# Placing a modulation's steps, the order of block couples, and the order of loads in the two MLPs of a fused block kernel

## The chip, the cores and the metric

The kernel runs on one core of a Trainium2 chip. A core has five engines with a queue of instructions each: PE (TensorE, matrix products), DVE (VectorE), ACT (ScalarE), POOL (GpSimd) and SP (SyncE, which here only issues DMAs). The metric is the time of one execution on the device in microseconds; lower is better. Several executions are timed and the median is given. A trace was taken of one of them.

## The reference, cut to what matters

Two transformer blocks follow each other on x of shape (1, 1024, 1024), all in float32. What the change touches is the MLP of each block, and the modulation vector of the second block:

```
# end of the first block
h = rmsnorm(x, g_mlp)
x = x + square(relu(h @ w_mlp_in)) @ w_mlp_out      # (1024,1024)x(1024,4096), (1024,4096)x(4096,1024)
x = rmsnorm(x, g_final)

# second block
mod = silu(c_2) @ w_ada_2 + b_ada_2                 # one row of 6 * 1024, cut in six:
sh1, sc1, gt1, sh2, sc2, gt2 = split(mod, 6)
x = x + gt1 * mixer(rmsnorm(x, g_mix_2) * (1 + sc1) + sh1)
h = rmsnorm(x, g_ffn_2) * (1 + sc2) + sh2
x = x + gt2 * (square(relu(h @ w_ff1_2)) @ w_ff2_2)
out = rmsnorm(x, g_final_2)
```

`mod` depends on inputs alone. It is first needed where the second block's first norm is made, at the end of the first MLP.

## The kernel before, in words

**Products.** Each float32 operand is split into a rounded part `hi` and a rest `lo` (`parts_of` for weights: a cast on ACT to `wh`, then a subtract on DVE, or on POOL where `eng=G`, to `wl`). `product` (L1231) adds up hi·hi, hi·lo and lo·hi over four chunks of 128: 12 matmuls of 128x128 by 128x512 into one PSUM bank.

**First GEMM of an MLP** (`mlp`, L1211). The hidden width of 4096 is cut into 16 couples m of two blocks of 128, the tokens into two halves of 512. A couple by two halves is a 2x2 block product, made in Winograd's form with seven products instead of eight. P1 and P2 (`first_two`, L1264) need only the first token half: P1 lands in `s1` (ACT copies it out), P2 plus `s1` gives `q11`, which is squared after a relu. The other five need operands made of both halves: T1 (in the place of the second half's first chunks), B22, and `t2`, `t3`, `t4` (six tiles of tag `q`). `make_t` (L1104) makes them on DVE, ACT and POOL when the second half's norm is known; its last part, `rest`, is called between two couples and holds four of the six PSUM banks. The norm itself comes from `begin[0]` (sum of squares, then a power on POOL, L127) and `begin[1]` (`spread`, L1035: four small PE transposes that lay the factor over the partitions).

Order in the code: P1, P2 of couples 0, 1, 2, with `begin[0]` and `begin[1]` between them, then `rest`, then couple 3; couples 2 and 3 split their weights on POOL. Then a loop over m: P5, then P1 and P2 of couple m + 1 (from m = 3 on), t2, B22, t3 and t4's products. `s1s` and `q11s` hold four couples. `sums` (L1279) makes the weights' sums of the next couple on POOL. Seven results per couple go to DRAM from ACT's queue (`save`).

**Modulation.** `ada` (L1182) is a Python generator: each `next` traces one step. For each of 12 column groups, eight steps load 128x512 of `w_ada_2` on SP's queue (`adaw`, two buffers) and multiply and add it on DVE into `ada`; then one empty step; then four PE transposes, a reduce and an add. `tick` calls it, only in the first MLP: four times per couple in the loop (L1312, L1331), once after it, and three times between products of the second GEMM (`tick2`, L1382).

**Second GEMM** (L1425). The hidden width comes in four quarters, each a 2x2 block product of seven products by four 128-wide blocks. `quarter` loads 1 MB of weights into a `q` tile, `second` loads 1 MB of stored results and splits it in four chunks (cast on ACT, subtract on DVE and POOL in turn, L1371). `upd` (L1374) adds a product to x, whose value was stored to DRAM before the MLP and is loaded back at L1356 in sixteen pieces, traced before all else of this stage. `U` and `V7` gather sums that are used twice. The x tiles are the same memory as `s1s`, `q11s` and the first GEMM's other results.

**What sets the order.** A planner of the framework lays the traced instructions out into one queue per engine: at each point it takes, of the instructions that its own estimate of time holds to be ready, the one traced first. So an instruction may be queued ahead of others traced before it, if it is thought ready sooner. Each engine then runs its queue strictly in that order, waiting on semaphores. A tile of a pool with n buffers can be given out again when the last reader of the tile n before it is done. `tc.issue_after(ins)` adds to each instruction traced inside it, on `ins`'s engine, the rule that it stands behind `ins` in the queue; it doesn't wait for `ins` to end.

Of the kernel before, what the change touches and what calls it, by code (L numbers as in the profile page):

```python
# [14 lines left out]
AF = mybir.ActivationFunctionType  # L15
# [4 lines left out]
P = 128  # L20
# [40 lines left out]
def block_kernel(ctx, tc, x, mem, positions, g_mix, w_in, b_gate, sinks, g_mem, w_mem_kv, w_proj_swa, w_proj_dsa,  # L61
# [50 lines left out]
    def tp_bank():  # L112
        return bank("tp")
# [1032 lines left out]

    xT = [hB([P, DC, 512], tag=n) for n in ("h_hi", "h_lo")]
# [30 lines left out]

    mod = cst([P, 48], tag="mod")
    bada = cst([P, 48], tag="bada")  # L1180

    def ada(modp):  # L1182
        badr = modp([48, P], tag="badr")
        nc.scalar.dma_start(badr, b_ada_2[0].rearrange("(k p) -> k p", p=P))
        pt = tp_bank()
        T.transpose(pt[:, :48], badr, ident[:48, :48])
        V.tensor_copy(bada, pt[:, :48])
        r0, _ = ROWS["c_2"]
        s_ = modp([P, 64], tag="silu")[:, :DC]
        A.activation(s_, cols[:, r0:r0 + 8], AF.Tanh, scale=0.5)  # L1190
        V.scalar_tensor_tensor(s_, s_, 1.0, cols[:, r0:r0 + 8], op0=OP.add, op1=OP.mult)
        V.tensor_scalar(s_, s_, 0.5, None, op0=OP.mult)
        for g in range(12):
            acc = modp([P, 512], tag="ada", bufs=1)
            for k in range(DC):
                w = modp([P, 512], tag="adaw", bufs=2)
                nc.sync.dma_start(w, w_ada_2[0, k * P:(k + 1) * P, halves(g)])
                if k == 0:
                    V.tensor_scalar(acc, w, s_[:, 0:1], None, op0=OP.mult)
                else:  # L1200
                    V.scalar_tensor_tensor(acc, w, s_[:, k:k + 1], acc, op0=OP.mult, op1=OP.add)
                yield
            yield
            m4 = mod[:, g * 4:(g + 1) * 4]
            pt = tp_bank()
            for j in range(4):
                T.transpose(pt[:, j * P:(j + 1) * P], acc[:, j * P:(j + 1) * P], ident)
            V.tensor_reduce(m4, pt.rearrange("p (j q) -> p j q", j=4), axis=AX.X, op=OP.add)
            V.tensor_tensor(m4, m4, bada[:, g * 4:(g + 1) * 4], op=OP.add)

    def mlp(PB, xt, d, w1, w2, scale, post, begin, middle, tick=lambda: None, gains=None, each=lambda i, e: None,  # L1211
# [52 lines left out]
        def first_two(m, e1, mid=None, eng=None):  # L1264
# [5 lines left out]
            if mid:  # L1270
                mid()
# [17 lines left out]
        first_two(0, w_of(wp, 0, "wr", 2))  # L1289
        begin[0]()  # L1290
        first_two(1, w_of(wp, 2, "wr", 2), begin[1])
        first_two(2, w_of(wp, 4, "wr", 2), eng=G)
        rest_t.pop()()
        begin[2]()
        first_two(3, w_of(wp, 6, "wr", 2), eng=G)
        e1s[0] = w_of(wep, 0, "we", 2)
        sums(0)
        for m in range(NM):
# [18 lines left out]
            V.tensor_tensor(q12, a, q12, op=OP.add)  # L1317
# [13 lines left out]
            for _ in range(2):  # L1331
                tick()
            a = mm_bank()
            product(a, u4, TQ["t4"])
            V.tensor_tensor(u3, a, u3, op=OP.add)
# [15 lines left out]
        tick()  # L1351
# [22 lines left out]
        def upd(hf, e, a, sl=slice(0, 512)):  # L1374
            t_ = xt[hf][:, e, sl]
            if scale is None:
                V.tensor_tensor(t_, a, t_, op=OP.add)
            else:
                V.scalar_tensor_tensor(t_, a, scale[:, e:e + 1], t_, op0=OP.mult, op1=OP.add)  # L1379
            return t_  # L1380

        def tick2():  # L1382
            for _ in range(3):
                tick()

        def gather(to, a, ch):
            if ch:
                V.tensor_tensor(to, a, to, op=OP.add)
            else:
                A.copy(to, a)  # L1390
# [34 lines left out]
        for ch in range(4):  # L1425
# [29 lines left out]
            tick2()  # L1455
# [13 lines left out]
            tick2()  # L1469
# [7 lines left out]
            tick2()  # L1477
# [8 lines left out]
            tick2()  # L1486
            if not last:
                b = second("q22", ch)
                for e, wt in blocks(a12):
                    a = mm_bank()  # L1490
                    product(a, wt, b)
                    upd(1, e, a)
                tick2()
# [39 lines left out]
    def post_mlp1(hf, st):  # L1533
        if hf == 0:
            for _ in ada_["it"]:
                pass
# [26 lines left out]
    ada_ = {}  # L1563

    def begin1():
        stp.close()
        ada_["it"] = ada(pools["mod"])
# [4 lines left out]
    def tick1():  # L1572
        next(ada_["it"], None)

    pools["mod"] = Pool("modp")
    mlp(hBp, xT, mlp_d, w_mlp_in[0], w_mlp_out[0], None, post_mlp1,
        (lambda: next(pend), lambda: next(pend), begin1), middle1, tick1, gsq)
    pools["mod"].close()
# [112 lines left out]
    pools["stm"].close()  # L1691
    pt = tp_bank()
# [405 lines left out]
```

## Time and profile before

| what | value |
|---|---|
| time, median of 3 (range) | 2725.16 us (2717.71 to 2726.5) |
| the profiled execution's own time | 2721.95 us |
| its span in the trace | 2720.2 us, 34915 instructions |
| PE, DVE, ACT, POOL busy | 2528.9, 1882.7, 1197.9, 988.1 us |
| mean granted clock of TensorE | 0.972 |
| first MLP in the trace | about 880 to 1610 us |
| second MLP in the trace | about 2037 us to the end |

Busy times are sums over the span; they overlap. Where PE is busy without a gap nothing else can shorten the time; where it is not, the idle time's releaser says what it waited for. A matmul's shown duration overlaps the next one's; how many of them fit into a stretch is the better measure.

### The profile page before, as it was taken

The page shows a single profiled execution, that of the slowest core. Times are in us where ns is not written, and L with a number is a line of the kernel's source. Part 1 is how long each engine was busy: PE and PEld are TensorE (multiplying, and loading weights), DVE is VectorE, ACT ScalarE, POOL GpSimd, SP SyncE. Part 2 cuts the span into 40 slices and gives each one's busy share as a digit, 9 for nine tenths or more (in the row PEclk, how much of TensorE's full clock was granted, in tenths as well). Part 3 has the DMA queues.
Part 4 walks back from the last instruction along what each step waited for, and adds up shares of the span by engine and source line. Part 5 has one row for each costly group of instructions (what it writes and reads, how often), then busy time and mean ns, then how long its engine had stood idle before and what let it go on. Part 6 is the DMA issues. An engine that isn't in the chain of part 4 may idle for free. (4 is left out here: it accounts for less than half of the span.)

```text
span 2720.2 us, 34915 instructions
## 1 busy us (share of the span) xinstructions
PE 2528.9 (93%) x12560; PEld 2107.4 (77%) x12560; DVE 1882.7 (69%) x3206; ACT 1197.9 (44%) x2218; POOL 988.1 (36%) x717
## 2 busy tenths in 40 slices
PE   7999999899999678888899979999997999989997
PEld 6899987788878566667688856888786788768886
DVE  7685878834455866676778896755658565578898
ACT  6575765335334433334433333323335554543433
POOL 3011123421002533333755661211334443476554
PEclk9999999999999889999999989999998999999999
DMA  3121022321155266666644301422343444753431
GB/s 114 53 61 40 25 79 90 89 61 41 63 183 179 78 203 200 202 204 230 220 170 155 109 24 51 156 63 70 120 152 97 160 150 159 250 204 134 170 109 62
DMA packets 275712, 338.57 MB, mean 124 GB/s; under 512 B 14268, under 2 KB 185044, under 8 KB 268372
## 3 DMA queue, kind: packets, MB, share of 16 engines
q1 hardware_dynamic: 234820, 253.65, 29.2%
q10 hardware_dynamic: 40720, 82.70, 8.3%
q8 instruction: 99, 1.62, 0.2%
q14 instruction: 73, 0.60, 0.1%
HBM read 250.25 MB, written 86.05 MB: 124 GB/s over the span
## 5 line engine op out<-in xcount | busy, mean ns | idle before, releaser
L1233 PE MATMUL mm<-h_hi,wh 128*128 128x512 f32 (+1 forms) x1136 | 455.5, 401 | 33.3 <-ACT wh L1227 17.2
L1235 PE MATMUL mm<-h_hi,wl 128*128 128x512 f32 (+1 forms) x1136 | 452.1, 398 | 10.5 <-DVE wl L1228 10.5
L1234 PE MATMUL mm<-h_lo,wh 128*128 128x512 f32 (+1 forms) x816 | 322.2, 395 | 0.0
L1233 PEld LDWEIGHTS mm<-h_hi,wh 128*128 128x128 f32 x1136 | 221.4, 195 | 82.2 <-ACT wh L1227 20.6
L1235 PEld LDWEIGHTS mm<-h_hi,wl 128*128 128x128 f32 x1136 | 220.7, 194 | 63.4 <-DVE wl L1228 18.2
L1227 ACT CAST wh<-q 128x1024 fp32r<-128x1024 f32 x116 | 121.7, 1052 | 331.7 <-PE mm L1234 297.7
L1234 PE MATMUL mm<-h_hi,wh 128*128 128x512 f32 (+1 forms) x624 | 244.8, 392 | 13.2 <-POOL h_hi L1371 13.2
L1228 DVE TENSOR_TENSOR wl<-q,wh 128x1024 fp32r<-128x1024 f32 x116 | 162.9, 1405 | 32.9 <-ACT wh L1227 31.3
L1234 PEld LDWEIGHTS mm<-h_lo,wh 128*128 128x128 f32 x816 | 158.3, 194 | 31.6
L1371 POOL TENSOR_TENSOR h_hi<-h_lo,h_hi 128x512 fp32r<-128x512 f32 x76 | 128.6, 1712 | 113.1 <-ACT h_hi L1370 107.9
L133 ACT CAST wh<-wr 128x1024 fp32r<-128x1024 f32 (+5 forms) x107 | 97.2, 911 | 149.7 <-PE mm L418 43.5
L1233 PE MATMUL mm<-q,wh 128*128 128x512 f32 x384 | 151.3, 394 | 10.4 <-DVE q L1119 10.4
L1235 PE MATMUL mm<-q,wl 128*128 128x512 f32 x384 | 150.2, 392 | 8.0 <-DVE wl L1228 8.0
L1234 PE MATMUL mm<-q,wh 128*128 128x512 f32 x384 | 150.9, 393 | 0.0
L1234 PEld LDWEIGHTS mm<-h_hi,wh 128*128 128x128 f32 x624 | 120.5, 193 | 37.9 <-POOL h_hi L1371 14.4
L1284 POOL TENSOR_TENSOR sa<-wr 128x512 f32<-128x512 f32 x32 | 41.7, 1303 | 264.8 <-DMA wr<-in_w_ff_dram 60.5
L134 POOL TENSOR_TENSOR wl<-wr,wh 128x1024 fp32r<-128x1024 f32 (+5 forms) x40 | 78.1, 1958 | 160.7 <-ACT wh L133 159.2
L1615 PE MATMUL mm<-h_hi,wh 128*128 128x512 f32 x320 | 132.0, 412 | 0.8 <-DVE kn L1648 0.8
L1617 PE MATMUL mm<-h_hi,wl 128*128 128x512 f32 x320 | 126.7, 396 | 0.0
L1371 DVE TENSOR_TENSOR h_hi<-h_lo,h_hi 128x512 fp32r<-128x512 f32 x76 | 120.4, 1605 | 8.3 <-ACT h_hi L1370 8.3
L1616 PE MATMUL mm<-h_lo,wh 128*128 128x512 f32 x320 | 125.5, 392 | 0.0
L1233 PE MATMUL mm<-h_lo,wh 128*128 128x512 f32 (+1 forms) x304 | 115.4, 380 | 0.6 <-ACT wh L1227 0.6
(589 smaller groups left out, 7006.9 us busy)
## 6 DMA issues: line engine op xcount, KB each, us to landing
h_lo<-ml_t SPq DMA_DIRECT2D x32, 1024.0 KB
adaw<-in_w_ada_dram SPq DMA_DIRECT2D x96, 256.0 KB
h_lo<-ml_q SPq DMA_DIRECT2D x24, 1024.0 KB
wr<-in_w_in_dram SPq DMA_DIRECT2D x42, 512.0 KB
wr<-in_w_out_dram SPq DMA_DIRECT2D x32, 512.0 KB
ml_t<-h_lo ACTq DMA_DIRECT2D x64, 256.0 KB
q<-in_w_mlp_out_dram SPq DMA_DIRECT2D x16, 1024.0 KB
ml_t<-x ACTq DMA_DIRECT2D x64, 256.0 KB
```

What stands on the lines that cost most here:

```text
L133: A.copy(hi, r)
L134: (eng or V).tensor_tensor(lo, r, raw(hi), op=OP.subtract)
L1227: A.copy(hi, r)
L1228: (eng or V).tensor_tensor(lo, r, raw(hi), op=OP.subtract)
L1233: mm(a, wt[0][:, k], b[0][:, k, sl], start=(k == 0), stop=False)
L1234: mm(a, wt[0][:, k], b[1][:, k, sl], start=False, stop=False)
L1235: mm(a, wt[1][:, k], b[0][:, k, sl], start=False, stop=(k == 3))
L1284: G.tensor_tensor(sa[:, 0:4], e2[:, 0:4], e2[:, 4:8], op=OP.add)
L1371: (G if c % 2 else V).tensor_tensor(lo[:, c], r[:, c], raw(hi[:, c]), op=OP.subtract)
L1615: mm(a, hi[:, k, :], r_hi, start=(k == 0), stop=False)
L1616: mm(a, hi[:, k, :], r_lo, start=False, stop=False)
L1617: mm(a, lo[:, k, :], r_hi, start=False, stop=(k == DC - 1))
```

## The change

It has four parts. (1) `ada` is moved up in the code and its pool opened earlier; its first two `next`s come in the projection before the first MLP, its loads are traced two steps ahead of their use, and each later `tick` gets an eviction on DVE and stands behind it. In the loop there are again four per couple, one behind each of four evictions; the other ticks follow evictions of the second GEMM's first three quarters. (2) P1 and P2 of couples 4, 5 and 6 come first, ahead of 0; their `s1` and `q11` go to DRAM (`away`) and are loaded back one iteration before their use; couples 0, then 1, 2, 3 follow, these three behind `rest`. Only couple 6 splits its weights on POOL. (3) In the second GEMM's first quarter the weights and the first two stored operands are traced ahead of the loads of x, which are four of 1 MB now. (4) In that quarter x is updated from the copied `U`, not from PSUM.

```diff
+        d["away"] = pool([P, 3, 2, 512], tag="ml_a")
...
     def ada(modp):
         badr = modp([48, P], tag="badr")
         nc.scalar.dma_start(badr, b_ada_2[0].rearrange("(k p) -> k p", p=P))
+        yield
...
+        yield
+        ld = []
+
+        def load(i):
+            if i < 12 * DC:
+                w = modp([P, 512], tag="adaw", bufs=2)
+                nc.sync.dma_start(w, w_ada_2[0, (i % DC) * P:(i % DC + 1) * P, halves(i // DC)])
+                ld.append(w)
+
+        load(0)
+        load(1)
         for g in range(12):
             acc = modp([P, 512], tag="ada", bufs=1)
             for k in range(DC):
-                w = modp([P, 512], tag="adaw", bufs=2)
-                nc.sync.dma_start(w, w_ada_2[0, k * P:(k + 1) * P, halves(g)])
+                w = ld.pop(0)
                 if k == 0:
                     V.tensor_scalar(acc, w, s_[:, 0:1], None, op0=OP.mult)
                 else:
                     V.scalar_tensor_tensor(acc, w, s_[:, k:k + 1], acc, op0=OP.mult, op1=OP.add)
+                load(g * DC + k + 2)
                 yield
...
+    def tick1(after):
+        with tc.issue_after(after.ins):
+            next(ada_, None)
...
         A.copy(xT[hf][:, e, :], pt)                      # x_cols, called for hf in 0, 1
+        if e == 2:
+            next(ada_)
...
             V.tensor_tensor(q11, a, s1, op=OP.add)       # first_two
             relu2(q11)
+            if away:
+                nc.scalar.dma_start(d["away"][:, m - 4, 0, :], s1)
+                nc.scalar.dma_start(d["away"][:, m - 4, 1, :], q11)
...
-        first_two(0, w_of(wp, 0, "wr", 2))
+        first_of(4, away=True)
         begin[0]()
-        first_two(1, w_of(wp, 2, "wr", 2), begin[1])
-        first_two(2, w_of(wp, 4, "wr", 2), eng=G)
+        first_of(5, away=True)
+        begin[1]()
+        first_of(6, eng=G, away=True)
+        first_of(0)
         rest_t.pop()()
         begin[2]()
-        first_two(3, w_of(wp, 6, "wr", 2), eng=G)
+        first_of(1)
+        first_of(2)
+        first_of(3)
...
-                if m >= 3:
+                if m >= 6:
                     first_two(m + 1, e1s[m + 1])
+                elif m >= 3:
+                    for i, t_ in enumerate((s1s, q11s)):
+                        nc.sync.dma_start(t_[(m + 1) % 4], d["away"][:, m - 3, i, :])
...
-            V.tensor_tensor(q12, p5, u2, op=OP.add)
-            for _ in range(2):
-                tick()
+            tick(V.tensor_tensor(q12, p5, u2, op=OP.add))
...
-            V.tensor_tensor(q12, a, q12, op=OP.add)
+            tick(V.tensor_tensor(q12, a, q12, op=OP.add))
...
-            V.tensor_tensor(q22, p5, u3, op=OP.add)
+            tick(V.tensor_tensor(q22, p5, u3, op=OP.add))
...
-            V.tensor_tensor(u3, a, u3, op=OP.add)
+            tick(V.tensor_tensor(u3, a, u3, op=OP.add))
...
-        for hf, es in ((1, range(4)), (0, range(8)), (1, range(4, 8))):
-            for e in es:
-                nc.sync.dma_start(xt[hf][:, e, :], d["x"][:, e, halves(hf)])
+        def x_back():
+            for hf, e0 in ((0, 0), (0, 4), (1, 0), (1, 4)):
+                nc.sync.dma_start(xt[hf][:, e0:e0 + 4, :], d["x"][:, e0:e0 + 4, halves(hf)])
...
+            if not late_ and e % 4 != 1 and (hf or e < 4):   # upd
+                tick(r)
...
+                if to is V7[0] or to is V7[2]:               # gather, from the second quarter on
+                    tick(r)
...
             b = second("q12", ch)
+            if not ch:
+                bt = second("t1", ch)
+                x_back()
             for e, wt in blocks(a11):
                 a = mm_bank()
                 product(a, wt, b)
                 gather(U[e], a, ch)
-                upd(1, e, a)
+                upd(1, e, a if ch else U[e])
             a12 = quarter(ch, 1, 0)
-            tick2()
-            b = second("t1", ch)
+            b = second("t1", ch) if ch else bt
...
-                V.tensor_tensor(U[e], a, U[e], op=OP.add)    # after t2's product
+                r = V.tensor_tensor(U[e], a, U[e], op=OP.add)
+                if e != 1:
+                    tick(r)
```

## Rows read from the trace of the kernel before

**Rows 1.** The page, part 1: busy us (share of the span) xinstructions.

```profile
PE 2528.9 (93%) x12560; PEld 2107.4 (77%) x12560; DVE 1882.7 (69%) x3206; ACT 1197.9 (44%) x2218; POOL 988.1 (36%) x717
```

**Rows 2.** Windows: length, busy us (count) of PE, PEld, DVE, ACT, POOL; PEclk, DMA share, GB/s.

```profile
880.00:930.00 50.00, 28.00 (x112) 21.77 (x111) 41.15 (x57) 23.41 (x40) 23.07 (x15) 0.79 0.24 74
930.00:1003.00 73.00, 59.22 (x247) 47.74 (x247) 52.84 (x63) 23.69 (x35) 33.67 (x22) 0.89 0.56 185
1003.00:1287.00 284.00, 252.05 (x1046) 198.04 (x1044) 200.84 (x261) 116.44 (x175) 102.15 (x72) 0.96 0.62 205
1287.00:1330.00 43.00, 27.96 (x102) 21.40 (x102) 23.03 (x23) 16.61 (x25) 30.88 (x14) 0.84 0.76 268
1330.00:1406.00 76.00, 76.00 (x337) 62.94 (x336) 63.09 (x65) 31.30 (x47) 46.97 (x23) 1.00 0.45 161
1406.00:1482.00 76.00, 76.00 (x337) 62.90 (x337) 64.43 (x65) 29.18 (x43) 45.50 (x22) 1.00 0.42 151
...
2037.00:2080.00 43.00, 27.03 (x114) 20.96 (x113) 37.92 (x51) 27.86 (x47) 21.01 (x14) 0.84 0.21 62
2080.00:2136.00 56.00, 52.76 (x217) 42.11 (x217) 32.59 (x39) 22.80 (x33) 30.44 (x22) 0.94 0.48 153
2136.00:2369.00 233.00, 232.92 (x1028) 192.55 (x1026) 132.25 (x164) 121.27 (x177) 100.49 (x73) 1.00 0.52 174
2369.00:2400.00 31.00, 19.51 (x67) 14.41 (x68) 17.29 (x17) 12.58 (x19) 23.07 (x11) 0.85 0.73 263
```

**Rows 3.** Waits of PE, 1003 to 1287: who waited for whom, total us, times, longest.

```profile
PE mm L1235 <- DVE wl L1228: 14.2, 16, 1.9
```

**Rows 4.** Waits of DVE, 1003 to 1287.

```profile
DVE ada L1201 <- DMA adaw<-in_w_ada_dram: 52.0, 30, 4.1
```

**Rows 5.** Groups of DVE, 1055 to 1230: count, busy us, mean ns, idle before, releaser.

```profile
L1201 DVE SCALAR_TENSOR_TENSOR ada<-adaw,silu,ada 128x512 f32<-128x512 f32 x50 | 40.5, 810 | 40.2 <-DMA adaw<-in_w_ada_dram 39.8
...
L1209 DVE TENSOR_TENSOR mod<-mod,bada 128x4 f32<-128x4 f32 x7 | 8.7, 1249 | 0.0
...
L1310 DVE TENSOR_TENSOR h_hi<-mm,h_hi 128x512 f32<-128x512 f32 x8 | 5.5, 684 | 0.0
```

**Rows 6.** Timeline of SP's queue: start us, us, what, count (merged).

```profile
1092.93 10.26 SPq L1197 DMA_DIRECT2D adaw<-in_w_ada_dram  x5
```

**Rows 7.** Timelines of ACT and DVE at the second MLP's start.

```profile
2051.79 1.05 ACT L1227 CAST wh<-sa 128x1024 fp32r<-128x1024 f32 x1
...
2080.54 1.20 DVE L1228 TENSOR_TENSOR wl<-sa,wh 128x1024 fp32r<-128x1024 f32 x1
```

**Rows 8.** Timelines of DVE, POOL and PE at the first MLP's start.

```profile
891.48 1.23 DVE L126 TENSOR_SCALAR st_r<-st_b 128x4 f32<-128x4 f32 x1
...
889.11 1.71 POOL L1284 TENSOR_TENSOR sa<-wr 128x512 f32<-128x512 f32 x1
...
897.96 1.02 POOL L127 TENSOR_TENSOR st_r<-st_r,mhalf 128x4 f32<-128x4 f32 x1
...
899.03 1.12 PE L1035 MATMUL tp<-ident,st_r 128*128 128x128 f32 x4 [10.23 <-POOL st_r L127]
```

**Rows 9.** Waits of PE, 1287 to 1330, and timelines of SP and ACT ahead of it.

```profile
PE mm L1234 <- POOL h_hi L1371: 7.4, 1, 7.4
PE mm L1233 <- ACT wh L1227: 6.0, 1, 6.0
...
1284.91 0.47 SPq L1407 DMA_DIRECT2D q<-in_w_mlp_out_dram  x1
...
1291.90 1.04 ACT L1227 CAST wh<-q 128x1024 fp32r<-128x1024 f32 x1 [7.49 <-DMA q<-in_w_mlp_out_dram]
```

**Rows 10.** Tile `ada`, 880 to 1345: duration ns min/median/max, first and last start.

```profile
L1201 DVE SCALAR_TENSOR_TENSOR ada<-adaw,silu,ada x84: 732/752/1803, 888.0 to 1232.2; 128x512 f32<-128x512 f32 x84
```

**Rows 11.** Groups of DVE and of POOL, 1330 to 1482.

```profile
L1371 DVE TENSOR_TENSOR h_hi<-h_lo,h_hi 128x512 fp32r<-128x512 f32 x19 | 33.7, 1799 | 0.0
...
L1450 POOL TENSOR_TENSOR q<-q,q 128x1024 f32<-128x1024 f32 x4 | 12.4, 3120 | 0.0
```

More of the change, by code (lines that the diff above doesn't have):

```diff
@@ L1145, in make_t, with ada @@
         rest_t.append(rest)
+    mod = cst([P, 48], tag="mod")
+    bada = cst([P, 48], tag="bada")
+    def ada(modp):
+        badr = modp([48, P], tag="badr")
+        nc.scalar.dma_start(badr, b_ada_2[0].rearrange("(k p) -> k p", p=P))
+        yield
+        pt = tp_bank()
+        T.transpose(pt[:, :48], badr, ident[:48, :48])
+        V.tensor_copy(bada, pt[:, :48])
+        r0, _ = ROWS["c_2"]
+        s_ = modp([P, 64], tag="silu")[:, :DC]
+        A.activation(s_, cols[:, r0:r0 + 8], AF.Tanh, scale=0.5)
+        V.scalar_tensor_tensor(s_, s_, 1.0, cols[:, r0:r0 + 8], op0=OP.add, op1=OP.mult)
+        V.tensor_scalar(s_, s_, 0.5, None, op0=OP.mult)
+        yield
[7 more added lines that the diff above has]
+        load(1)
+        for g in range(12):
+            acc = modp([P, 512], tag="ada", bufs=1)
+            for k in range(DC):
+                w = ld.pop(0)
+                if k == 0:
+                    V.tensor_scalar(acc, w, s_[:, 0:1], None, op0=OP.mult)
+                else:
+                    V.scalar_tensor_tensor(acc, w, s_[:, k:k + 1], acc, op0=OP.mult, op1=OP.add)
+                load(g * DC + k + 2)
+                yield
+            yield
+            m4 = mod[:, g * 4:(g + 1) * 4]
+            pt = tp_bank()
+            for j in range(4):
+                T.transpose(pt[:, j * P:(j + 1) * P], acc[:, j * P:(j + 1) * P], ident)
+            V.tensor_reduce(m4, pt.rearrange("p (j q) -> p j q", j=4), axis=AX.X, op=OP.add)
+            V.tensor_tensor(m4, m4, bada[:, g * 4:(g + 1) * 4], op=OP.add)
+    modp = Pool("modp", side="right")
+    ada_ = ada(modp)
+    def tick1(after):
+        with tc.issue_after(after.ins):
+            next(ada_, None)
     xT = [hB([P, DC, 512], tag=n) for n in ("h_hi", "h_lo")]
@@ L1176, in block_kernel, with mlp @@
     HT[1] = h_tiles(hBp)
[L1179 to L1195, printed above, removed]
-                w = modp([P, 512], tag="adaw", bufs=2)
-                nc.sync.dma_start(w, w_ada_2[0, k * P:(k + 1) * P, halves(g)])
[L1198 to L1211, printed above, removed]
+    def mlp(PB, xt, d, w1, w2, scale, post, begin, middle, tick=lambda ins: None, gains=None, each=lambda i, e: None,
             parts=((0, 0, 512), (1, 0, 512))):
@@ L1262, in save_later, with first_two @@
                 save(*later.pop(0))
-        def first_two(m, e1, mid=None, eng=None):
+        def first_two(m, e1, eng=None, away=False):
             s1, q11 = s1s[m % 4], q11s[m % 4]
@@ L1287, in sums, with first_of @@
             G.tensor_tensor(e1[:, 4:8], e1[:, 4:8], sa[:, 4:8], op=OP.subtract)
-        first_two(0, w_of(wp, 0, "wr", 2))
+        def first_of(m, **kw):
+            first_two(m, w_of(wp, 2 * m, "wr", 2), **kw)
+        first_of(4, away=True)
         begin[0]()
-        first_two(1, w_of(wp, 2, "wr", 2), begin[1])
-        first_two(2, w_of(wp, 4, "wr", 2), eng=G)
+        first_of(5, away=True)
+        begin[1]()
+        first_of(6, eng=G, away=True)
+        first_of(0)
         rest_t.pop()()
         begin[2]()
-        first_two(3, w_of(wp, 6, "wr", 2), eng=G)
+        first_of(1)
+        first_of(2)
+        first_of(3)
         e1s[0] = w_of(wep, 0, "we", 2)
@@ L1327, in mlp @@
             V.tensor_tensor(u3, a, u2, op=OP.add)
-            V.tensor_tensor(q22, p5, u3, op=OP.add)
+            tick(V.tensor_tensor(q22, p5, u3, op=OP.add))
             relu2(q22)
             save("q22", m, q22)
-            for _ in range(2):
-                tick()
             a = mm_bank()
             product(a, u4, TQ["t4"])
-            V.tensor_tensor(u3, a, u3, op=OP.add)
+            tick(V.tensor_tensor(u3, a, u3, op=OP.add))
             A.activation(u3, u3, AF.Relu)
@@ L1376, in upd @@
             if scale is None:
-                V.tensor_tensor(t_, a, t_, op=OP.add)
+                r = V.tensor_tensor(t_, a, t_, op=OP.add)
             else:
-                V.scalar_tensor_tensor(t_, a, scale[:, e:e + 1], t_, op0=OP.mult, op1=OP.add)
-            return t_
-        def tick2():
-            for _ in range(3):
-                tick()
+                r = V.scalar_tensor_tensor(t_, a, scale[:, e:e + 1], t_, op0=OP.mult, op1=OP.add)
+            if not late_ and e % 4 != 1 and (hf or e < 4):
+                tick(r)
+            return t_
         def gather(to, a, ch):
             if ch:
-                V.tensor_tensor(to, a, to, op=OP.add)
+                r = V.tensor_tensor(to, a, to, op=OP.add)
+                if to is V7[0] or to is V7[2]:
+                    tick(r)
             else:
@@ L1534, in post_mlp1 @@
         if hf == 0:
-            for _ in ada_["it"]:
+            for _ in ada_:
                 pass
@@ L1561, in h2_half @@
         yield
-    ada_ = {}
     def begin1():
         stp.close()
-        ada_["it"] = ada(pools["mod"])
     def middle1():
         pools["stm"] = Pool("stm", side="right", n512=2)
-    def tick1():
-        next(ada_["it"], None)
-    pools["mod"] = Pool("modp")
     mlp(hBp, xT, mlp_d, w_mlp_in[0], w_mlp_out[0], None, post_mlp1,
         (lambda: next(pend), lambda: next(pend), begin1), middle1, tick1, gsq)
-    pools["mod"].close()
     drm.close()
@@ L1691, in block_kernel @@
     pools["stm"].close()
+    modp.close()
     pt = tp_bank()
```

8 lines of the change are left out of this document (removed).

## The prediction

> **What bounds the kernel now.** I read the page first, then windows cut at the stages of the two MLPs, then the waits of PE and DVE inside them, then timelines at the two starts and the two hand-overs. PE is busy 93% of the span [rows 1], so a change pays only where PE is not. The windows [rows 2] say where that is: in the second GEMM PE runs 337 matmuls in 76.00 us without a gap, 0.2255 us each. That is my unit: a stretch has lost its length less 0.2255 us per matmul.
>
> The first GEMM is one computation done twice. The first MLP, from 930 to 1287, has 247 + 1046 PE instructions in 357 us; 48 are the small transposes of the modulation, so 1245 matmuls or 280.7 us: 76 us lost. The second MLP, from 2080 to 2369, runs the same 217 + 1028 = 1245 in 289 us: 8 us lost. Only the first carries the modulation steps, so these and what follows from them cost 76 - 8 = 68 us. PE waits there for weight splits of DVE [rows 3], and DVE in turn has stood 52.0 us, 30 times, at the head of its queue for `adaw` from DRAM, 4.1 us at worst [rows 4]. In 175 us (seven couples) DVE made 50 accumulating steps, over seven a couple [rows 5]: nothing ties a step to its place in the code, where two ticks stand twice per couple, so the planner took each as soon as it thought the load done, ahead of evictions.
>
> Four other losses, by the same unit with the small transposes left out [rows 2]: the starts (880 to 930 and 2037 to 2080) some 27 and 19 us, and the hand-overs to the second GEMM (1287 to 1330: 43 - 102 x 0.2255 = 20; 2369 to 2400: 31 - 67 x 0.2255 = 16).
>
> **The change part by part.**
>
> *Steps behind evictions, loads two steps ahead.* A couple gets four steps, each queued behind an eviction; the transposes come two ticks after the last step. Does a step still wait for its load? With two buffers SP issued five loads in 10.26 us while DVE waited [rows 6], four intervals of 2.5 us; a buffer's turn is two, 5.1 us, less a step of 0.8, so about 4.3 us from issue to landing. Load i+2 goes out after step i, and step i+2 stands two products, 2 x 2.7 = 5.4 us, later at the closest. It lands with 1.1 us to spare, and more across the next couple's P5, P1 and P2. So I take DVE's 52 us as gone.
>
> What is late next? In the second MLP's steady part DVE is busy 132.25 of 233 us, 57%, or 10.8 us of a couple of 84 matmuls (19 us) [rows 2]. Four steps of 0.81 and 0.44 of a reduce (taken as an eviction, 0.68) and an add (1.25) make 4.1 us more [rows 5]: 14.9 of 19, so PE stays the bound. I allow 0.8 us a couple for the transposes and jitter, over nine such couples 7 us. The other six couples (m = 0 to 5) now lack P1 and P2: 60 matmuls, 13.5 us of PE, and DVE, less a split (1.20, [rows 7]) and an eviction, 10.8 - 1.9 + 4.1 = 13.0. In the second MLP three such couples without steps lost 56 - 217 x 0.2255 = 7 us [rows 2], 2.4 each; with steps I take 2.9, for six 17 us. Left are 24 of 76 us: **-52**. Bounds: -68 (nothing left but the 8) and -22 (the short couples at 6 us each and 2 us on the long).
>
> *P1 and P2 of couples 4, 5, 6 first, three couples back through DRAM.* The work is only moved; it pays if it fills the stall before the operands T1 to T4. That stall is DVE's: it is busy 41.15 of 50 and 37.92 of 43 us there [rows 2]. Before, four couples could run in it: two whose subtracts DVE did earlier, two split on POOL. After, 4 and 5 are split on DVE, 6 on POOL, 0 on DVE, all traced ahead of the rest of make_t; 1, 2 and 3 behind it, split on DVE. That is the point on which it turns. In the second MLP `sa` had its cast at 2051.79 and its subtract only at 2080.54 [rows 7], after nearly all of make_t: what is traced later gets no place on DVE until then. So 1, 2 and 3 come after the stall, and as many couples as before run inside it: **0** in the second MLP at the start, and **+3** for its three more short couples (1 us each; the 7 us above hold the first one's filling). If the subtracts slip in, each MLP gains up to three couples of 24 matmuls, 16 us; if they delay make_t, it costs their 6 us.
>
> At the first MLP's start there is something to gain. POOL's pow ran at 897.96 behind the four sums for m = 0, begun at 889.11, and a split on POOL; its input was ready at 892.7; PE stood 10.23 us until the spread at 899.03 [rows 8]. After, those sums follow seven couples, and the silu and first `ada` steps no longer sit on DVE ahead of that input. The spread then waits only for PE's own second couple, at about 880 + 48 x 0.2255 = 891 plus the transposes: **-7** (0 to -10).
>
> Spills: six stores on ACT's queue and six loads on SP's, 256 KB each, per MLP. The first GEMM's DMA share is 0.62 at 205 GB/s with seven steps a couple; four steps take away more than the reloads add. I price them at nothing; what hides them is a whole couple between a reload and its use.
>
> *Second GEMM's loads first.* PE stood 6.0 us for the cast of the first weights and 7.4 us for a chunk that POOL split after its sums [rows 9]. SP issued `q` at 1284.91, behind loads of x; the cast waited for it until 1291.90. Now the weights and two operands go ahead of x, and the second operand's split precedes those sums in the code. But the weights' buffers are T2's and T3's, free only with the last products, so I take half of 20 + 16: **-18** (-30 to 0). The first updates now wait for x in DVE's queue; U is copied out on ACT first, so no bank hangs on it.
>
> *Steps left for the second GEMM.* 111 resumptions: 2 early, 64 in the loop, 45 left: 18 in the first quarter, 20 in the second, 7 in the third. DVE has 76 - 63.09 = 12.9 and 76 - 64.43 = 11.6 us free there [rows 2]. It gets 16 x 0.81 + 2 x 1.93 = 16.8 and 18 x 0.81 + 3.9 = 18.5: over by 3.9 and 6.9: **+11**. From below 0, since six banks buffer. From above, with each step at the longest seen, 1.803 us [rows 10], 19.8 + 24.8 = 45.
>
> Sum: -52 + 0 + 3 - 7 - 18 + 11 = -63. The profiled execution took 2721.95 us (span 2720.2), 3.2 under the median shown, so it stands for it: 2721.95 - 63 = 2659, and I say **2660**.
>
> **The rivals.**
>
> *The extra couples do run in the stall.* For it: PE idles there and ACT has room; against it: rows 7. Some 14 us in each MLP: 2660 - 28 = 2632.
>
> *The second GEMM's DVE is too full.* A step reads two SBUF tiles and meets POOL, busy 46.97 of 76 us [rows 2], with sums of 3.12 us; DVE's own 128x512 subtracts beside POOL's take 1.80 us [rows 11], and such a step 0.752 at the median [rows 10]. If a step waits for the POOL instruction under way, 0.62 x 1.2 (half of 2.4, between 1.8 and 3.12) is 0.75 more: 1.55 a step. First quarter 16 x 1.55 + 3.9 - 12.9 = 15.8, second 18 x 1.55 + 3.9 - 11.6 = 20.2; 36 for 11: 2685. The Trainium skill ("SBUF — State Buffer", Who interferes with whom) has the rule: a Vector instruction with two SBUF inputs and a GpSimd one that reads SBUF hold a port in turn, each for its whole length. The 1.80 us agree; but the median of the steps, taken beside less POOL work, does not yet show it.
>
> *The order of loads buys nothing,* because buffers and not the queue hold the first weights: 18 us back, 2678. For it: `q` went out 3 us before the last product ended.
>
> *Slower: steps tied to a place wait for late landings.* If landing takes over 5.4 us, every second step of a couple (about 28) and all 39 of the second GEMM stand in DVE with evictions behind them. From (63 / 67) = 0.94 us each, that is 6.4 us to land, the whole gain is gone; at 7 us it is 67 x 1.6 = 107 - 63: 2766. For it: the DMA share of 0.62 [rows 2], and shorter couples; against it: about 4.3 us now.
>
> **How the numbers follow.** Forecast 0.50, extra couples in the stall 0.20, DVE too full 0.16, loads no gain 0.09, late landings 0.05. The range takes in the first four with part of their spread: **2620 to 2703**. 0.3% is 8 us, about what can be told from no change: faster (under 2717) 0.94, same 0.02, slower 0.04, the last two from the late landings and a pile-up of the bounds.
>
> **What would show it.** Right: no wait of DVE for `adaw` above some 10 us in total; long couples 19 to 20 us apart in the first MLP; the first spread at about 892; `ada` steps into the third quarter of the first MLP's second GEMM, and PE gaps there. Wrong: PE busy with couples 1 to 3 between the spread and the end of make_t; couples of 60 matmuls at 13.5 us; DVE still waiting for `adaw`, which would break the largest term.

## The result, and the profile after

After: 2685.89 us, median of 4 (2682.84 to 2690.99), against 2725.16; ratio 0.9863 (of means), 95% interval 0.984 to 0.9887. So 39 us were gained where 65 were forecast; the range held. The profiled execution of after is 5.1 us above its median, that of before 3.2 below, so the two traces differ by 30.9 us only (spans 2689.3 and 2720.2).

The page, part 1, as in [rows 1]:

```profile
PE 2523.5 (94%) x12560; PEld 2106.1 (78%) x12560; DVE 1904.6 (71%) x3208; ACT 1198.8 (45%) x2218; POOL 981.6 (37%) x715
```

Windows of after, columns as in [rows 2]: the first MLP's start, its first GEMM, the first three quarters of its second GEMM, then the second MLP's short couples (60 matmuls) and long ones (84).

```profile
880.00:930.00 50.00, 37.30 (x147) 29.19 (x146) 39.21 (x56) 26.49 (x45) 12.14 (x10) 0.80 0.32 98
930.00:1237.00 307.00, 283.81 (x1231) 231.83 (x1229) 229.02 (x270) 139.49 (x207) 143.28 (x98) 0.97 0.64 207
1237.00:1337.00 100.00, 84.78 (x343) 67.33 (x344) 78.93 (x74) 37.54 (x57) 59.08 (x27) 0.90 0.72 256
1337.00:1420.00 83.00, 78.83 (x349) 63.79 (x348) 83.00 (x93) 28.63 (x43) 47.94 (x23) 1.00 0.60 209
1420.00:1502.00 82.00, 78.52 (x342) 64.64 (x341) 71.27 (x74) 29.45 (x43) 47.26 (x24) 0.98 0.42 144
...
2073.00:2140.00 67.00, 61.85 (x260) 49.16 (x259) 32.48 (x44) 27.62 (x40) 30.17 (x24) 0.97 0.58 193
2155.00:2340.00 185.00, 184.24 (x812) 151.87 (x810) 111.60 (x133) 96.93 (x145) 79.57 (x59) 1.00 0.52 176
```

Read PE's count against the length. The first GEMM is shorter, but the second and third quarters of the second one, without a gap before, now take 83 and 82 us, and in the second quarter DVE is busy all 83. In 67 us of the second MLP's short couples PE loses 67 - 260 x 0.2255 = 8 us; in the long ones next to nothing.

For a finer account I cut every trace by PE's own products: G1 is the first GEMM, from its first to its last matmul (1344); Q0 from there through a quarter (336 matmuls) of the second, Q1 and Q2 the next quarters. a and b are the first and second MLP; the time is the median, beside its ratio to before.

| kernel | G1a | Q0a | Q1a | Q2a | G1b | Q0b | time | ratio, interval |
|---|---|---|---|---|---|---|---|---|
| before | 406.7 | 96.8 | 76.2 | 76.2 | 330.8 | 93.0 | 2725.16 | 1 |
| after | 353.9 | 104.4 | 82.7 | 81.9 | 336.1 | 90.7 | 2685.89 | 0.9863, 0.984 to 0.9887 |
| e1_leave | 353.4 | 95.4 | 76.2 | 76.2 | 335.1 | 89.9 | 2663.09 | 0.9778, 0.9757 to 0.98 |
| e2_spread | 368.5 | 100.5 | 76.7 | 76.7 | 335.4 | 91.5 | 2689.24 | 0.9867, 0.9852 to 0.9882 |
| e3_noload | 352.6 | 106.4 | 80.5 | 80.3 | 335.7 | 91.2 | 2687.2 | 0.9861, 0.9847 to 0.9876 |
| e4_fill | 340.8 | 102.7 | 80.6 | 81.9 | 330.0 | 89.6 | 2667.4 | 0.9787, 0.9768 to 0.9805 |
| e5_oldx | 350.5 | 101.2 | 82.6 | 81.9 | 336.0 | 94.5 | 2689.45 | 0.9875, 0.9861 to 0.989 |
| e6_oldc | 347.2 | 103.0 | 81.0 | 81.7 | 330.6 | 91.3 | 2674.3 | 0.9821, 0.9806 to 0.9836 |
| e7_tie | 348.3 | 102.3 | 82.4 | 81.9 | 336.1 | 90.7 | 2680.15 | 0.9842, 0.9826 to 0.9858 |
| e8_all | 338.4 | 103.4 | 76.7 | 76.7 | 327.2 | 91.6 | 2658.01 | 0.9759, 0.9744 to 0.9775 |
| e9_t1dve | 342.7 | 102.2 | 82.4 | 81.9 | 322.0 | 90.3 | 2662.91 | 0.9783, 0.9767 to 0.9799 |
| e10_best | 331.4 | 103.1 | 76.7 | 76.7 | 317.9 | 90.9 | 2640.39 | 0.9693, 0.9677 to 0.9709 |
| e11_old | 344.2 | 102.6 | 76.7 | 76.7 | 330.3 | 88.8 | 2665.81 | 0.9789, 0.9774 to 0.9805 |
| e12_t1sp | 359.6 | 102.3 | 81.0 | 80.3 | 333.9 | 89.3 | 2686.49 | 0.9863, 0.9847 to 0.988 |

A cell of one trace moves by some 2 us where nothing was changed (Q0a is 104.4 in after and 102.3 in e12; Q1a 82.7 and 81.0). Each kernel's ratio is to runs of before taken beside its own (medians 2720.8 to 2725.26 us), so between kernels the ratios compare better than the times.

### The profile page after: what moved, and what is told of

Same layout as the page of the kernel before. It is cut to its first block, busy times and chain, and to the rows that moved or that the text cites. A ratio compares the mean times of both kernels' runs of the same rounds, so it can differ in the third digit from the quotient of the medians.

```text
span 2689.3 us, 34920 instructions
## 1 busy us (share of the span) xinstructions
PE 2523.5 (94%) x12560; PEld 2106.1 (78%) x12560; DVE 1904.6 (71%) x3208; ACT 1198.8 (45%) x2218; POOL 981.6 (37%) x715
## 5 line engine op out<-in xcount | busy, mean ns | idle before, releaser
L1250 DVE TENSOR_TENSOR wl<-q,wh 128x1024 fp32r<-128x1024 f32 x116 | 181.0, 1562 | 28.7 <-ACT wh L1249 27.4
L1257 PE MATMUL mm<-h_lo,wl 128*128 128x512 f32 (+1 forms) x304 | 117.5, 386 | 7.2 <-DVE wl L1250 7.2
L1250 DVE TENSOR_TENSOR wl<-we,wh 128x1024 fp32r<-128x1024 f32 x50 | 83.4, 1668 | 57.6 <-ACT wh L1249 53.5
```

The lines of the kernel that those rows point to most:

```text
L1250: (eng or V).tensor_tensor(lo, r, raw(hi), op=OP.subtract)
L1257: mm(a, wt[1][:, k], b[0][:, k, sl], start=False, stop=(k == 3))
```

## The experiments

All edits are to after.

**e1_leave: the steps in the second GEMM, left out.** Five of the twelve groups of `mod` are not computed.

```diff
+        n_tick[0] += 1
+        if n_tick[0] > 64:
+            return
         with tc.issue_after(after.ins):
```

> The changed kernel without the modulation steps that it still has to do after the first GEMM: the first 64 ticks are made, the other 45 (39 multiply-adds with their loads, five sets of transposes, reduces and adds) are left out, and so are five of the twelve column groups of mod. In the changed kernel the first MLP's second GEMM took 99.3, 82.7 and 81.9 us for its first three quarters, against 90.4, 76.2 and 76.2 before. Theory A (DVE is too full there, steps included): the quarters fall to about 88, 76.2 and 76.2, and the time by 20 to 22 us, to some 2665. Rival B (SP's queue: loads of adaw wait for a step and hold up operand loads behind them): the same here. Rival C (the new order of the first quarter's loads is what costs): 99, 76, 76, so about 12 us less and the first quarter stays long.

Q0a, Q1a and Q2a fall by 9.0, 6.5 and 5.7 us, 21.2 together; the time by 22.8. The first quarter falls less than theory A's 11. The steps left over are the whole loss of these quarters (19 rather than 21 us if the 102.3 of e7 and e12 is the truer Q0a of after). Without them Q0a is 95.4 against 96.8 before: so much the new order of loads can have given the first MLP. Theory A and rival B are not told apart here; e3 does that. The window of e1's second quarter, to be laid beside 83.00 of 83.00 above:

```profile
1330.00:1405.00 75.00, 75.00 (x333) 62.10 (x332) 63.45 (x64) 29.18 (x42) 44.36 (x23) 1.00 0.44 154
```

**e3_noload: the steps kept, their last 38 loads left out** (they read the last loaded tile again).

```diff
-            if i < 12 * DC:
+            if 57 < i < 12 * DC:
+                ld.append(w_at[0])
+            elif i <= 57:
```

> The changed kernel with all its modulation steps on DVE in their places, but without the loads of the last 38 of the 96 weight tiles: those steps read the last loaded tile again, so the second GEMM has the DVE work and none of the adaw transfers; mod's last five groups come out wrong by that. Theory A (DVE's time): the quarters stay within 2 us of 99.3, 82.7 and 81.9. Rival B (SP's queue held up by adaw loads that wait for their buffer's last step): about 90, 77, 77 and a time some 18 us lower. A mixture shows as a first quarter that falls and later ones that don't.

Q1a and Q2a are 2.2 and 1.6 us lower, hardly more than in e12, which has all the loads (81.0 and 80.3); Q0a is not lower, and DVE is still never idle in the second quarter (third busy figure):

```profile
1337.00:1418.00 81.00, 78.42 (x349) 64.13 (x348) 81.00 (x89) 29.61 (x44) 47.03 (x23) 1.00 0.42 143
```

So it is DVE's time that is short in the second quarter, not the loads, though in after SP stood 110.2 us, 34 times, at loads waiting for a step to free their buffer (1225 to 1510):

```profile
SPq L1170 <- DVE ada L1182: 110.2, 34, 14.8
```

The first quarter is another matter: DVE has free time in it. Its windows in after and in e1, with TensorE's granted clock (a mean over its levels of 1.2 and 2.4 GHz) third from the end:

```profile
1232.00:1337.00 105.00, 86.28 (x352) 68.39 (x351) 83.59 (x80) 39.17 (x59) 62.58 (x30) 0.90 0.73 263
1230.00:1326.00 96.00, 83.71 (x345) 66.86 (x344) 73.54 (x64) 38.30 (x59) 66.77 (x32) 0.93 0.69 259
```

There PE waits 6.9 us for weight splits on DVE against 3.0 in e1, and 2.5 us for the small transposes; the clock is lower too. Which of these the steps cause, and how, no run separates.

**e2_spread: more steps in the first GEMM.** Six per couple from couple 6 on, some ten per quarter of the second GEMM.

```diff
+            r = V.tensor_tensor(q11, a, s1, op=OP.add)
+            if m >= 7:
+                tick(r)
...
+            r = V.tensor_tensor(t2_, q21, t1_, op=OP.subtract)
+            if m >= 6:
+                tick(r)
...
-            if not late_ and e % 4 != 1 and (hf or e < 4):
+            if not late_ and e in (0, 2):
```

> The changed kernel with the ticks dealt out anew: six per couple from m = 6 on (added behind the adds of q11 and of t2_), four per couple before that, ten per quarter of the second GEMM instead of 18 and 20, so that three quarters share 28 or so. Theory A: each quarter has 11.6 to 12.9 us of DVE free and now gets 10 x 0.8 to 1.3 and some 2 of reduces, so the quarters fall to about 92, 78 and 78, while the long couples of the first GEMM rise from 19.0 to at most 19.3 us (DVE 10.8 + 6 x 0.81 + 1.2 = 16.9 of 19): some 14 us less than the changed kernel. Rival B expects less, 5 us, as loads of adaw still stand in SP's queue in all three quarters.

The quarters are mended (76.7 twice), but G1a grows by 14.6 us and the time stays. The rows that tell why are PE's waits in the first GEMM, of e2 (930 to 1240) and then of after (880 to 1237):

```profile
PE tp L1189 <- DVE ada L1182: 26.5, 5, 8.5
PE mm L1257 <- DVE wl L1250: 1.9, 2, 1.4
```

```profile
PE tp L1189 <- DVE ada L1182: 15.7, 3, 8.6
PE mm L1255 <- ACT h_hi L1291: 6.4, 1, 6.4
PE mm L1255 <- DVE q L1120: 5.7, 1, 5.7
PE mm L1257 <- DVE wl L1250: 3.5, 3, 2.4
PE mm L1255 <- ACT wh L1249: 1.1, 2, 0.8
```

PE stands at the modulation's small transposes, for the last step of a group. The change ties a step to an eviction on DVE; the transposes that follow it are PE's and are tied to nothing, so they stand in PE's queue ahead of products.

**e7_tie: the transposes tied too.**

```diff
-            for j in range(4):
-                T.transpose(pt[:, j * P:(j + 1) * P], acc[:, j * P:(j + 1) * P], ident)
+            with tc.issue_after(last_mm[0].ins):
+                for j in range(4):
+                    T.transpose(pt[:, j * P:(j + 1) * P], acc[:, j * P:(j + 1) * P], ident)
```

> The changed kernel with the four small transposes of each group of twelve queued, on PE, behind the last matmul of the product whose eviction carries them; in the changed kernel they hang on nothing but their operand `ada`. Theory (they stand in PE's queue ahead of their place, and PE stops for the last step of the group): the 15.7 us that PE stood for `ada` in three places of the first MLP's first GEMM go, that GEMM falls from 353.9 us to 340-346, the second GEMM's quarters stay (104.4, 82.7, 81.9), and the whole comes to about 2675 us. Rival (DVE is what is late there, and the transposes only show it): PE stands as long at the next weight split; first GEMM 352-355, whole 2684-2688.

PE's wait at the transposes falls from 15.7 to 3.1 us (same stretch of e7), but its wait for casts of weights grows from 1.1 to 9.8:

```profile
PE mm L1256 <- ACT wh L1250: 9.8, 5, 4.4
PE mm L1256 <- ACT h_hi L1292: 6.7, 1, 6.7
PE mm L1258 <- DVE wl L1251: 6.4, 7, 2.4
PE mm L1256 <- DVE q L1120: 5.7, 1, 5.7
PE tp L1190 <- DVE ada L1182: 3.1, 1, 3.1
```

G1a gains 5.6 us, about half of the theory's 8 to 14, and the intervals of the two times overlap.

**e4_fill: couples 1 and 2 ahead of the rest of the operands, split on POOL.**

```diff
         first_of(0)
+        first_of(1, eng=G)
+        first_of(2, eng=G)
         rest_t.pop()()
         begin[2]()
-        first_of(1)
-        first_of(2)
         first_of(3)
```

> The changed kernel with couples 1 and 2 traced ahead of the rest of make_t and split on POOL, couple 3 after it on DVE. My theory says that couples 1 to 3 came after the stall because their subtracts stand behind make_t in DVE's order: then this puts two couples, 48 matmuls or 10.9 us, into the idle stretch of each MLP (the two gaps of 6.4 and 5.7 us in the first, 6.8 and 4.6 in the second, nearly vanish), and make_t ends 1 to 3 us later for two more evictions. Expected: 14 to 18 us less in all, 7 to 9 in each MLP. Rival: the PSUM banks are short (make_t holds four of six), so make_t starts later and the couples push the operands back by what they gain: 0 to 4 us less.

18.5 us faster, as the theory had it for the whole, though not in its parts: G1a by 13.1, G1b by 6.1. In after PE stood 5.7 us for `q`, an operand of the second half (the rows of after just above e7's edit); here it is 0.5 us (waits of PE, 880 to 930 of e4):

```profile
PE mm L1255 <- ACT h_hi L1291: 5.5, 1, 5.5
PE mm L1255 <- DVE q L1120: 0.5, 1, 0.5
```

The waits fall by 6 to 7 us, but the first 168 matmuls take 44.7 us where they took 57.0. Most of the rest is the granted clock: after's PE stands 6.4 and 5.7 us in short order and has 0.82 in the stretch, e4's has 0.98, and the same 177 PE instructions are busy 4.8 us less (windows of after, then of e4):

```profile
879.00:936.00 57.00, 44.30 (x177) 34.98 (x176) 43.88 (x60) 31.30 (x52) 17.85 (x13) 0.82 0.30 91
879.00:924.00 45.00, 39.51 (x177) 32.38 (x177) 35.15 (x45) 29.56 (x48) 26.47 (x18) 0.98 0.37 114
```

The earlier place and the split on POOL were changed together and are not told apart.

**e5_oldx: loads of the second GEMM as before** (x first in sixteen pieces, the second operand after the first product's chunk, first updates from PSUM).

```diff
+        for hf, es in ((1, range(4)), (0, range(8)), (1, range(4, 8))):
+            for e in es:
+                nc.sync.dma_start(xt[hf][:, e, :], d["x"][:, e, halves(hf)])
...
-                bt = second("t1", ch)
-                x_back()
```

> The changed kernel with the hand-over to the second GEMM as before: x loaded first, in sixteen pieces, the second operand loaded after the first product's chunk, the first updates reading PSUM. Theory (the order of the loads is worth little; buffers and the split of the first weights set the hand-over): from the end of the first GEMM's products through the second GEMM's first quarter the second MLP goes from 90.7 to about 93 us, the first from 104.4 to 106, the whole from 2686 to 2688-2692. Rival (the forecast's 18 us were gained, and the steps beside them hid it): each hand-over loses 8-10 us, whole 2701-2706.

2689.45, 3.6 us above after, the intervals overlapping. Q0b loses 3.8 us; Q0a does not (101.2 to 104.4). In the second MLP (2325 to 2375) the old wait for POOL's split is back, as in [rows 9]:

```profile
PE mm L1256 <- POOL h_hi L1400: 7.4, 1, 7.4
PE mm L1255 <- ACT wh L1249: 2.9, 1, 2.9
```

**e6_oldc: couples in the old order,** 0 to 3 first, 4 to 6 inside the loop, nothing through DRAM, couples 2 and 3 split on POOL again.

```diff
-        first_of(4, away=True)
+        first_two(0, w_of(wp, 0, "wr", 2))
...
-                if m >= 6:
+                if m >= 3:
                     first_two(m + 1, e1s[m + 1])
```

> The changed kernel with couples 0 to 3 first and 4 to 6 inside the loop, as before, and nothing through DRAM. Theory (the moved couples bring nothing in the stall and lose some 2 us each as short couples; the order of POOL's sums gains at the first MLP's start): the second MLP's first GEMM goes from 336.1 back to 330-332; in the first MLP the start loses 8-11 us (first 168 matmuls 57.0 to 65-68) and the couples win some 5; whole 2684-2690. Rival (the moved couples fill part of the stall before the second half's operands): both first GEMMs get longer by 8 us or more, whole 2700 or more.

2674.3: without this part of the change the kernel is 11.6 us faster, better than either theory allowed. G1a is 6.7 shorter, G1b 5.5. The start is worse, as expected (POOL's pow holds PE again, waits of 880 to 930):

```profile
PE tp L1035 <- POOL st_r L127: 4.9, 1, 4.9
```

To the 168th matmul after is ahead of e6 by 4.7 us in the first MLP (57.0 against 61.7) and 2.8 in the second (56.1, 58.9). In the couples that follow it loses 11.4 and 8.3, which leaves it 6.7 and 5.5 behind.

**e9_t1dve: why a short couple takes 16.9 us and not 13.5.** In after's second MLP the last subtract on POOL comes at intervals of 17.0, 16.8, 16.9 and 16.7 us in couples 0 to 4, though 60 matmuls are 13.5. Timelines of POOL and ACT in one of them (start us, us, instruction):

```profile
2084.62 1.29 POOL L1307 TENSOR_TENSOR sa<-wr 128x512 f32<-128x512 f32 x1 [3.10 <-DVE wl L1250]
...
2088.61 1.30 POOL L1310 TENSOR_TENSOR we<-we,sa 128x512 f32<-128x512 f32 x1
2089.87 1.29 POOL L1351 TENSOR_TENSOR x<-x,x 128x512 f32<-128x512 f32 x1
```

```profile
2086.51 0.33 ACTq L1280 DMA_DIRECT2D ml_q<-x  x1
2091.19 0.33 ACTq L1280 DMA_DIRECT2D ml_t<-x  x1
2091.56 1.04 ACT L1249 CAST wh<-we 128x1024 fp32r<-128x1024 f32 x1 [5.08 <-POOL x L1351]
```

POOL makes t1 (L1351) after the four sums of a later couple's weights (L1307 to L1310); ACT stands at t1's store until then, and the cast of the next weights, which needs neither t1 nor these sums, is queued behind it: 5.08 us.

```diff
-            G.tensor_tensor(t1_, q11, q12, op=OP.subtract)
+            (V if m < 6 else G).tensor_tensor(t1_, q11, q12, op=OP.subtract)
```

> The changed kernel with one subtract per short couple (t1, couples 0 to 5) on DVE and not on POOL. Theory (a short couple is held by ACT: its queue stands up to 5 us at the store of t1, because POOL makes t1 only after the sums for the next couple, and the next cast of weights stands behind that store): the short couples of the second MLP fall from 16.9 us to 14-15, its first GEMM from 336.1 to 325-330, the first MLP's from 353.9 to 345-349, the whole to 2670-2676. Rival (the short couples are short of DVE, or of the two operations between p5 and the products, and POOL only shows it): both first GEMMs stay within 2 us or get longer, whole 2683-2692.

2662.91; G1a 11.2 and G1b 14.1 us shorter, more than the theory said. The intervals are 14.2, 13.7, 13.7 and 13.7 us, close to PE's own time, and PE runs without a gap there:

```profile
2058.00:2119.00 61.00, 61.00 (x271) 50.49 (x270) 45.95 (x55) 30.20 (x44) 33.14 (x21) 1.00 0.69 228
```

The same cast on ACT now waits 1.51 us:

```profile
2069.34 0.33 ACTq L1280 DMA_DIRECT2D ml_t<-x  x1
2069.70 1.05 ACT L1249 CAST wh<-we 128x1024 fp32r<-128x1024 f32 x1 [1.51 <-DVE x L1351]
```

So with t1 on DVE the moved couples come out ahead: e9's ratio is 0.9783, that of e6, the old order, 0.9821. The old order with t1 on DVE was not tried.

**e12_t1sp: only the store moved, to SP.**

```diff
-            nc.scalar.dma_start(d[n][:, m, :], t_)
+            (nc.sync if n == "t1" and m < 6 else nc.scalar).dma_start(d[n][:, m, :], t_)
```

> The changed kernel with the store of t1 of the short couples (0 to 5) issued by SP and not by ACT; POOL still makes t1, behind the sums. It tells apart what moving the subtract to DVE left together. Theory (only the store in ACT's queue holds the couple, not POOL's lateness as such): short couples of the second MLP fall from 16.9 to 14-15 us, its first GEMM to 322-329, the first MLP's to 343-349, whole 2663-2676. Rival (what POOL makes late holds the couple by itself, since t2 and t4 need t1, or SP's loads now stand behind the store): short couples 16 us or more, whole 2682-2692.

2686.49, no gain: the rival. Now SP stands at the store, and the loads behind it come late; ACT's casts then stand, by the profile, for a reload of a moved couple's values (2068 to 2135):

```profile
SPq L1280 <- POOL x L1351: 49.2, 4, 12.7
```

```profile
ACT wh L1249 <- DMA x<-ml_a: 20.5, 3, 7.9
```

The short couples take 16.2 to 16.5 us, but for the first interval (17.8) and the last (15.5). So a queue that holds the store stands until POOL has made t1, and pays with whatever is behind it. Whether a late t1 would hold the couple with a store on no busy queue was not tried.

**e8_all, e10_best, e11_old: put together.** e8 is e4, e7 and e2's spread in one; e10 adds e9's edit; e11 is e6 with tied transposes and the spread (five steps from couple 6).

> The changed kernel with three edits: couples 1 and 2 traced ahead of the rest of the operands and split on POOL; the small transposes tied behind a product; six steps a couple from couple 6 on, five or six per product block fewer in the second GEMM. Theory (the stall filled: -19 us, as measured alone; the transposes' waits, which made six steps a couple cost 14.6 us, gone; the steps taken out of the second GEMM give it 4, 6 and 5 us): first GEMM of the first MLP 335-342 us, quarters 100, 77, 77, whole 2640-2650. Rival (six steps a couple overload DVE in the first GEMM, transposes or not): that GEMM at 350 or more, whole 2655-2665.

> The three edits together (stall filled with couples 1 and 2 split on POOL; transposes tied behind a product; six steps a couple from couple 6) and t1 of the short couples on DVE. Theory: the gain of t1 on DVE adds to 2658 us: first GEMMs 328-333 and 318-322 us, whole 2640-2648. Rival (with the stall filled, POOL's splits and ACT's casts in it set the short couples' rhythm): within 4 us of 2658.

> The old order of couples (0 to 3 first, nothing through DRAM) with the transposes tied and five steps a couple from couple 6 on. Theory (leaving out the couples' part of the change gains 11 us; tied transposes and fewer steps in the second GEMM gain 6 and 10 more): first GEMM of the first MLP 341-346 us, of the second 331, second GEMM's second and third quarter 77, whole 2655-2662. Rival (POOL's sums ahead of the start and steps in the long couples take it back): 2668 or more.

e8: 2658.01. With the transposes tied, the two more steps per couple no longer lengthen G1a (338.4, against e4's 340.8), and Q1a and Q2a are down to 76.7. But Q0a did not gain, and the steps took most of what tying gains, so the time is the rival's, though its G1a of 350 is not. e10: 2640.39, as its theory had it, 80 us under before (2720.8 in its runs) and some 1.7% under after (0.9693 / 0.9863 = 0.983). e11 is 2665.81, 8.7 us by ratio under e6 and between its theory and its rival: G1a gained 3 us where 1 to 6 were expected, Q1a and Q2a 9.3 together.

## Why the prediction was right and where it was wrong

**Steps behind evictions: the mechanism was right, the term was -52.** DVE's waits for `adaw`, 52.0 us in [rows 4], are now (930 to 1240):

```profile
DVE ada L1182 <- DMA adaw<-in_w_ada_dram: 3.9, 3, 1.9
...
DVE ada L1180 <- DMA adaw<-in_w_ada_dram: 1.0, 1, 1.0
```

That is 4.9 us, under the 10 that the forecast allowed, so the rival of late landings is dead. e6, which has this part without the couples, shows G1a 59.5 us shorter than before, with 7.1 of it at the start (168 matmuls in 61.7 for 68.8): 52.4. That this meets the -52 is partly luck, for the term was made for the new order, with 17 us lost in six short couples. In after itself G1a behind its start is 297 us where it was 338, 41 shorter; with t1 on DVE (e9) it is 11 shorter still. I had not seen the transposes' own stop, 15.7 us in after, though before's trace has it as PE's largest wait from 850 to 1350, with 12.6 us of it in the window of [rows 3], beside the 14.2 for splits that I showed:

```profile
PE tp L1207 <- DVE ada L1201: 26.4, 9, 12.2
```

The long couples came out 19.0 to 20.0 us apart all the same, but for two of 21.3 and 21.6 (starts of t1's subtract).

**The first MLP's start: right in mechanism, gone in the sum.** The spread was to come at about 892, for a gain of 7. The pow no longer stands behind the sums, the spread comes at 890, and 168 matmuls take 57.0 us for 68.8; 7.1 of these 11.8 us e6 has too:

```profile
887.09 1.03 POOL L127 TENSOR_TENSOR st_r<-st_r,mhalf 128x4 f32<-128x4 f32 x1 [2.70 <-DVE st_r L126]
...
890.17 0.60 PE L1035 MATMUL tp<-ident,st_r 128*128 128x128 f32 x4
```

**Couples 1 to 3 in the stall: right that they don't run there.** Couple 1's subtract comes at the very end of make_t, as [rows 7] had it for `sa`:

```profile
922.70 1.21 DVE L1250 TENSOR_TENSOR wl<-wr,wh 128x1024 fp32r<-128x1024 f32 x1
...
923.84 0.68 DVE L1120 TENSOR_TENSOR q<-mm,q 128x512 fp32r<-128x512 f32 x1
```

e4 shows that their place in the code and the engine of the split, changed together there, kept them out, and not the stall itself.

**The short couples: wrong.** The step that failed is "+3 for its three more short couples (1 us each; the 7 us above hold the first one's filling)". I read 2.4 us of loss per short couple and explained most of it away as filling. It was the rhythm of the short couples: in the second MLP 16.9 - 13.5 = 3.4 us in each of four intervals (the fifth, up to couple 5, is 14.7), with ACT standing at the store of a late t1. The window of 67 us that shows 8 us lost hides part of it: four couples are 240 matmuls, and PE made 260, the rest left over from the couples before. The 2.9 us per short couple inside the -52 fell short by the same step. I priced DVE and PE for such a couple, and did not go through ACT's queue, where stores and casts share one order. The couples' part of the change, forecast at 0 + 3 - 7 = -4, costs 11.6 (e6): 16 us of the miss. Moving P1 and P2 out of a couple took away 5.4 us of PE work that covers the wait: in the second MLP's long couples (after, 2160 to 2340) ACT stands at t1's store as well, and PE has no wait at all.

```profile
ACT x L1276 <- POOL x L1351: 21.3, 8, 4.0
```

**The hand-overs: wrong in size.** "I take half of 20 + 16: -18." Measured: Q0b 93.0 to 90.7, and in the first MLP 96.8 to 95.4 without steps (e1); e5 puts the whole at 3.6 us in the time. The second MLP's wait for POOL's split did go (7.4 in e5), but most of the rest is set by something else than the order of loads; what, no run shows. (`q` went out 2 us before the last product ended, not 3.) The rival "the order of loads buys nothing" (18 us back) was nearly right: 14 us of the miss.

**Steps in the second GEMM: mis-sized, 21 for 11.** The second quarter was right: over by 6.9 in the sum, 6.5 measured. The third lost 5.7 for 0: steps ran on to 1446.6, some 27 us into it, so DVE's backlog was carried over, and I had counted each quarter for itself. The first lost 9.0 (or 7) for 3.9, and there DVE was not full (83.59 of 105 us): PE stood for late splits and for the transposes, which the sum of DVE's busy time doesn't see, and the clock was lower. How these share the loss stays open. The rival's price per step (1.55 us) was near for the step itself, in the second quarter of after:

```profile
L1250 DVE TENSOR_TENSOR wl<-q,wh 128x1024 fp32r<-128x1024 f32 x15 | 22.5, 1498 | 0.0
L1182 DVE SCALAR_TENSOR_TENSOR ada<-adaw,silu,ada 128x512 f32<-128x512 f32 x15 | 20.2, 1345 | 0.0
L1400 DVE TENSOR_TENSOR h_hi<-h_lo,h_hi 128x512 fp32r<-128x512 f32 x10 | 11.6, 1168 | 0.0
```

but not for the sum. Without steps, the ten splits of the last row's kind take 1889 ns each there (e1):

```profile
L1406 DVE TENSOR_TENSOR h_hi<-h_lo,h_hi 128x512 fp32r<-128x512 f32 x10 | 18.6, 1889 | 0.0
```

The steps meet POOL in place of the splits. DVE's total rose from 63.45 x 76.2 / 75 = 64.5 to 83.0, by 18.5 us, the forecast's own figure for this quarter (18 x 0.81 + 3.9). The Trainium skill's rule ("SBUF — State Buffer", Who interferes with whom: such instructions of the two engines take the shared port in turn) agrees with both rows. I read them so that a meeting is paid once per POOL instruction and not once per step; no run isolates that.

**The sum.** Misses of 16, 14 and 10 us, 40 in all, against a shortfall of 26 us. The other way stand the 7.5 us by which e6's G1a beat the -52 (7.1 of them at the start) and the 8.3 by which the two profiled executions sit off their medians. 2 us are left without a place. The forecast's mechanisms were mostly right, and its range held; the gain of the moved couples and most of that of the hand-overs were not there.

## What to carry to other kernels

When work is taken out of a loop body, go through every engine's queue of the shorter body, DMA issues included: a store waiting for a slow engine's result holds all that is queued behind it, and the work taken out may have been its cover (moving one subtract gave 22 us by ratio here). When a step is tied to a place on one engine, tie its followers on the other engines too. And where a background load is cut into stages, carry an engine's overload from one stage into the next instead of summing stages.

## What was not expected of the hardware

The accumulating steps on DVE run in 0.747 us at the median in the first GEMM and 1.161 in the second, 2.884 at worst (tile `ada` of after, 880 to 1237, then 1237 to 1502). POOL is busy beside them 47% of the time in the first GEMM and 58% in the second quarter of the second:

```profile
L1182 DVE SCALAR_TENSOR_TENSOR ada<-adaw,silu,ada x49: 735/747/1855, 944.9 to 1230.0; 128x512 f32<-128x512 f32 x49
```

```profile
L1182 DVE SCALAR_TENSOR_TENSOR ada<-adaw,silu,ada x35: 735/1161/2884, 1266.9 to 1446.6; 128x512 f32<-128x512 f32 x35
```

With that, one DVE instruction's time is no constant to multiply; in the second quarter the engine's total was nearer to one. Nor is one matmul's: filling a stall of PE paid 4.8 us in granted clock besides the wait (e4).
